# Two transformer blocks on one core: a later read of the bias table, plain float32 sums for the modulation, and the first activation on other engines

## The chip, the cores and the metric

The kernel runs on one core of one Trainium2 chip. The metric is the device time of one execution in microseconds (us). Five engines work beside each other, each in its own order: PE (TensorE, matrix products; the loading of its weights is listed as PEld), DVE (VectorE), ACT (ScalarE), POOL (GpSimd) and SP (SyncE, which here only issues transfers). ACT also issues a few transfers.

## The reference

Two blocks over 256 tokens of width 2048, all in float32. What the change touches is the head of the first block:

```python
c_act = jax.nn.silu(c)
mod = c_act @ w_ada[l] + b_ada[l]                     # 6 * 2048 columns
sh1, sc1, gt1, sh2, sc2, gt2 = jnp.split(mod, 6, axis=-1)
h = modulate(rms_norm(x, g_mix[l]), sh1, sc1)         # y * (1 + scale) + shift
z = h @ w_in[l]                                       # eleven parts
o_sb = stick_breaking_attention(...)
o_ds = indexer_sparse_attention(..., rel_bias)        # 8 heads
```

In the sparse attention an indexer of 16 heads scores all keys, the best 64 per query are kept, and every head adds a bias that depends on the distance of query and key (a table of 32 buckets). Then follow the output projections, a feed-forward part with a short convolution, and a second block with forgetting attention, sparse attention in three branches and a gated feed-forward part.

## The kernel before

**Weights.** All weights come once, in float32, in loads of up to 128x1024 elements (512 KB) that SP issues into a ring of `raw` buffers (line 268 for weights, line 271 for the modulation matrix `w_ada`). There are ten such buffers in the first projection and six from its last part on. A load of weights is split in two: ACT rounds it into a high half `wh` (line 295), DVE subtracts that from it to give the low half `wl` (line 302). Every product is then three passes on PE (high by high, high by low, low by high; lines 402 to 407 and 418 to 420), with the activation split in the same manner. The splitting runs three half-loads ahead of PE's products.

**Order.** The order of the work is written out by the program itself. A function `run` goes through the list of loads and emits the products; after every 1.27 us worth of matrix columns it makes one *tick*, which lets every running generator (norms, attention heads, modulation sums) emit its next step. `yield` in a generator waits for the next tick, `wait(n)` for n of them. So a later tick is a later place in every engine's queue.

**Modulation.** `mod` is computed in 28 chunks of 2 to 4 times 128 columns. The rows of `w_ada` are multiplied by `cact` and summed over the k-tiles, partly by DVE (line 329), partly by ACT and POOL (lines 326, 327), into two accumulators. The first two chunks go another way: plain float32 products on PE (lines 320 and 354). For the other 26 `ada_finish` (line 361) runs over several ticks: POOL adds the two accumulators (line 366), two ticks later ACT rounds the sum into a high half (line 368), a tick later DVE makes the low half (line 370), and 3 or 10 ticks after that PE sums over the partitions by multiplying with a column of ones (line 375), two products per 128 columns. `ada_put` (line 347) adds the bias of the layer.

**First activation.** The 16 k-tiles of `x` are handled in six parts of 2, 2, 3, 3, 3 and 3 (`KG`). The first projection goes over these parts one after the other, and adds the results of a part to those of the parts before: in turn DVE adds out of PSUM (lines 524, 526) or ACT copies (line 521) and POOL adds (line 522). While part j is multiplied, `h_prep(j + 1)` makes the next: `h_scale` multiplies by the norm factor `rb` (line 632, DVE), then it waits until the modulation columns are there, forms the gain (line 641, DVE), applies gain and shift per k-tile (line 645, DVE), and one tick later each ACT (line 656) and DVE (line 659) make the two halves.

**Bias table.** When the eight heads of the first attention are done, three generators start in the same tick: `bias_table`, `indexer` and `ds_chain` (line 1053). `bias_table` gathers the table, and at its end ACT issues one transfer that writes it to memory 128 times over (line 772, tile `tabs`, 8 x 128 x 384 elements, 1.57 MB, in rows of 1536 bytes). `ds_chain` waits until that generator has emitted its last step, then issues the read for head 0 (line 779, `bias_rows`, from ACT), waits for the indexer and starts the heads (`ds_head`, POOL adds the bias in lines 904 and 905). The indexer emits one head per tick (PE lines 803 and 804, ACT line 807, DVE line 813), then the selection of the best keys; it takes some 60 ticks.

Of the kernel before, what the change touches and what calls it, by code (L numbers as in the profile page):

```python
# [9 lines left out]
F32 = mybir.dt.float32  # L10
# [28 lines left out]
RA = (0.6, 0.7, 0.9, 0.9, 0.45)  # L39
GAPS = (5, 7)  # L40
KG = (2, 2, 3, 3, 3, 3)
KG0 = tuple(sum(KG[:j]) for j in range(len(KG)))
# chunks of the modulation's columns, (first, number), in units of 128
ADA = [(16 * m + k, n) for m in (0, 1) for k, n in zip(KG0, KG)] + [(c, 4) for c in range(32, 96, 4)]
# [77 lines left out]
def kernel(ctx: ExitStack, tc: tile.TileContext, t):  # L122
# [29 lines left out]
    invp = const.tile([128, 1], F32, name="invp")  # L152
    onesr = const.tile([128, 2], F32R, name="onesr")
    cact = const.tile([128, 16], F32, name="cact")
# [10 lines left out]
    class Pair:  # L165
        """an activation [128 * nk, T] as two parts whose sum it is, the two of a k-tile beside each other"""

# [11 lines left out]
        def part(self, i, k0, n):  # L179
            """high or low parts of k-tiles of one slot"""  # L180
            return self.slots[k0 // 4].rearrange("p (k i) n -> p i k n", i=2)[:, i, k0 % 4:k0 % 4 + n, :]
# [11 lines left out]
    def lut(func, **kw):  # L193
        """an activation of a table function; Exp and Ln out of the set that has both"""
        if func in (AF.Exp, AF.Ln) and tables[0] != "ln_exp":
            nc.scalar.add_instruction(mybir.InstLoadActFuncSet(
                name=nc.get_next_instruction_name(), act_func_set_id=LN_EXP, engine=mybir.EngineType.Activation,
                ins=[], outs=[]))
            tables[0] = "ln_exp"
        elif func not in (AF.Exp, AF.Ln):  # L200
            tables[0] = func
        nc.scalar.activation(func=func, **kw)  # L202

    # ---------------------------------------------------------------- stream of weights
    P = {}
# [28 lines left out]
    def pieces(n, width):  # L234
        """(first, number) of the k-tiles of every piece that a raw buffer holds"""
        m = -(-n // (RAW // width))
        return [(n * i // m, n * (i + 1) // m - n * i // m) for i in range(m)]
# [46 lines left out]
    def split(idx, g, ks, off, stage):  # L284
        """parts of a weight half, or of the modulation: what ScalarE does, then what VectorE does"""
        it, r = items[idx], raw_of[idx]
# [74 lines left out]
    def ada_finish(a):  # L361
        acc, w = ada_acc.pop(a), 128 * ADA[a][1]
        s = acc[:, 1, :w]
        hl = P.get("ft", ab).tile([128, 2, 512], F32R, name="adahl", tag="adahl", bufs=1)
        yield
        nc.gpsimd.tensor_tensor(out=s, in0=acc[:, 0, :w], in1=s, op=OP.add)
        yield from wait(2)
        nc.scalar.activation(out=hl[:, 0, :w], in_=s, func=AF.Copy)
        yield
        nc.vector.tensor_sub(out=hl[:, 1, :w], in0=s, in1=hl[:, 0, :w].bitcast(F32))  # L370
        yield from wait(FW[a // NKG if a < 2 * NKG else 2])
        ps = psm()
        for j in range(ADA[a][1]):
            for x in range(2):
                nc.tensor.matmul(ps[:, 2 * j:2 * j + 2], hl[:, x, 128 * j:128 * (j + 1)], onesr, start=(x == 0),
                                 stop=(x == 1))
        ada_put(a, ps, 2)

# [115 lines left out]

    # ---------------------------------------------------------------- helpers
    def alt():
# [11 lines left out]
    def gather(out_, ps):  # L508
        """the sum of a bank's halves"""
        nc.scalar.activation(out=out_, in_=ps[:, :T], func=AF.Copy)  # L510
        nc.vector.tensor_add(out=out_, in0=ps[:, T:], in1=out_)
# [36 lines left out]
    def rsqrt_of(out_, src, inv_n, w):  # L548
        """out = 1/sqrt(src * inv_n + eps)"""
        r0 = tmp.tile([128, T], F32, name="r0", tag="r0", bufs=1)[:, :w]  # L550
        m = tmp.tile([128, T], F32, name="mm", tag="mm", bufs=1)[:, :w]
        lut(out=r0, in_=src, func=AF.Ln, scale=inv_n, bias=epsc)
        lut(out=r0, in_=r0, func=AF.Exp, scale=-0.5)
        nc.vector.tensor_scalar(out=m, in0=src, scalar1=inv_n, scalar2=EPS, op0=OP.mult, op1=OP.add)
        nc.vector.tensor_mul(out=m, in0=m, in1=r0)
        nc.vector.tensor_mul(out=m, in0=m, in1=r0)
        nc.vector.tensor_scalar(out=m, in0=m, scalar1=-0.5, scalar2=1.5, op0=OP.mult, op1=OP.add)
        nc.vector.tensor_mul(out=out_, in0=r0, in1=m)
# [3 lines left out]

    # ---------------------------------------------------------------- block 1, attention
    poolA = ExitStack()
# [26 lines left out]
    nc.vector.memset(invp, 1.0 / 128)  # L591
    nc.scalar.activation(out=onesr, in_=ones[:, 0:2], func=AF.Copy)
    lut(out=cact, in_=V["c"], func=AF.Silu)
# [34 lines left out]

    def h_scale(j):
        for _, b, u, m in h_segs(j):  # L630
            x = xt[b][:, u, :]
            nc.vector.tensor_tensor(out=x, in0=x, in1=rb[:, None, :].to_broadcast([128, m, T]), op=OP.mult)

    def h_prep(j):
        """the modulated norm, k-tiles of part j"""
        k0, n = KG0[j], KG[j]
# [6 lines left out]
        for k in range(k0, k0 + n):  # L643
            x = xt[k // 8][:, k % 8, :]
            nc.vector.tensor_scalar(out=x, in0=x, scalar1=gain[:, k:k + 1], scalar2=mod[:, k:k + 1], op0=OP.mult,
                                    op1=OP.add)
            if j == 0:
                nc.scalar.activation(out=acts["h"](k)[0], in_=x, func=AF.Copy)
        if j == 0:
# [28 lines left out]

    # stick-breaking attention, one head
    def sb_head(h):  # L680
# [34 lines left out]
    def av_out(a, vs, o_pair, h, extra=None):  # L715
        """o^T = sum over sources of v^T a, with a in [keys, q] blocks"""
        O = psm()
# [21 lines left out]
    def seq(gens, gap):  # L739
        """start the generators one after the other, gap ticks apart, and go on until all are done"""  # L740
        mine = []
# [16 lines left out]

    # relative-position bias: bias_h[p, u] = table_h[127 - p + u], out of a copy of the table for every p
    tabs = dram.tile([8, 128, 384], F32, name="tabs")  # L760
# [20 lines left out]

    # indexer
    kix = ab.tile([128, T], F32, name="kix")
# [77 lines left out]
    def scores(q, k):  # L861
        """S[q, keys] = q^T k"""
        S = psm()
# [4 lines left out]
    def softmax(S, add, pool, shift=None):  # L868
        """p[q, keys] = exp(S + add + shift - max), with row sums"""
        p = pool.tile([128, 384], F32, name="t2", tag="t2")  # L870
# [48 lines left out]

    # ---- groups of block 1  # L920
    def f_evac(name, base, first=True, scale=None):
# [12 lines left out]
    def f_groups(tiles, nk, act, rmap, **kw):  # L934
        """groups of up to four feature tiles, each (weights, column, what takes its result)"""
        gs = []
# [116 lines left out]
    def ds_chain():  # L1053
        while gens["bias"] in active:
            yield
        rows_of[0] = bias_rows(0)
        while gens["ix"] in active:
            yield
        yield from seq([ds_head(h) for h in range(8)], GAPS[1])

# [76 lines left out]

    # ---------------------------------------------------------------- block 1, output projection and FFN
    def open_ffn(first):
# [14 lines left out]
    def x_out(k, g_ap, pair, accs):  # L1154
        """scaled copy of x chunk k as operand pair, and sums of squares"""
        x = xk(k)
# [208 lines left out]

    # ---------------------------------------------------------------- block 2, mixer
    R = {}
# [23 lines left out]
    def head_norm(z, gname, w=512):  # L1391
        """z[128, w] /= rms over the partitions, times the gain"""
        g = R["gcol"][:, GC[gname]:GC[gname] + 1]
# [52 lines left out]
    def ctok(j):  # L1446
        """kc or vc, and after its two heads the position embeddings of a block's halves"""
        return R["ck"].rearrange("p a n -> p (a n)")[:, 544 * j:544 * j + 544]
# [39 lines left out]
    def compress():  # L1488
        """weights of a block's halves beside each other times a row of every chunk, then the chunks' sums"""
        ws = {}  # L1490
# [38 lines left out]

    # compressed branch, all heads at once  # L1530
    def cmp_branch():
# [71 lines left out]

    # forgetting attention
    vf = get("vf", lambda: ring.tile([128, 2, 1024], F32, name="ringv", tag="ring"))
# [98 lines left out]

    # ---------------------------------------------------------------- block 2, output projection and FFN
    def on_act(k):
# [85 lines left out]
```

## Time and profile before

| what | us |
|---|---|
| three runs | 2840.61, 2840.67, 2844.85 |
| median | 2840.67 |
| span of the profiled execution, first to last instruction | 2837.6 |
| PE busy | 2732.4 (96%) |
| DVE busy | 2030.4 (72%) |
| ACT busy | 1431.9 (50%) |
| POOL busy | 831.5 (29%) |
| transfers | 590.45 MB, mean 208 GB/s |

The profiled execution's own time is not given apart from its span; the span leaves out what lies before the first and after the last instruction. A matmul's end is modelled, and products overlap, so a PE that is shown as busy can still lose time between them. [...] All times in the profile count from the first instruction.

### The profile page before, as it was taken

The page shows a single profiled execution, that of the slowest core. Times are in us where ns is not written, and L with a number is a line of the kernel's source. Part 1 is how long each engine was busy: PE and PEld are TensorE (multiplying, and loading weights), DVE is VectorE, ACT ScalarE, POOL GpSimd, SP SyncE. Part 2 cuts the span into 40 slices and gives each one's busy share as a digit, 9 for nine tenths or more (in the row PEclk, how much of TensorE's full clock was granted, in tenths as well). Part 3 has the DMA queues.
Part 4 walks back from the last instruction along what each step waited for, and adds up shares of the span by engine and source line. Part 5 has one row for each costly group of instructions (what it writes and reads, how often), then busy time and mean ns, then how long its engine had stood idle before and what let it go on. Part 6 is the DMA issues. An engine that isn't in the chain of part 4 may idle for free.

```text
span 2837.6 us, 47798 instructions
## 1 busy us (share of the span) xinstructions
PE 2732.4 (96%) x18364; PEld 2494.8 (88%) x18364; DVE 2030.4 (72%) x2851; ACT 1431.9 (50%) x2138; POOL 831.5 (29%) x703
## 2 busy tenths in 40 slices
PE   7899996989999999999999999999999999999999
PEld 7788885788988999989999888989998888888888
DVE  8999994988888996555666774676775665556654
ACT  5554563555655655434454543555554454344443
POOL 3766751456664541000101210111222221012210
PEclk9999998999999999999999999999999999999999
DMA  9787766778977875655555576544555555555554
GB/s 325 240 258 239 240 219 170 251 232 270 305 259 248 282 268 180 192 188 184 184 183 184 181 214 194 163 128 132 188 186 187 189 181 193 186 187 189 188 194 141
DMA packets 334944, 590.45 MB, mean 208 GB/s; under 512 B 21234, under 2 KB 85594, under 8 KB 334716
## 3 DMA queue, kind: packets, MB, share of 16 engines
q1 hardware_dynamic: 331236, 583.61, 63.3%
q10 hardware_dynamic: 3480, 3.79, 0.7%
q8 instruction: 144, 2.36, 0.3%
q14 instruction: 84, 0.69, 0.1%
HBM read 581.49 MB, written 5.78 MB: 207 GB/s over the span
## 4 chain that ended last, share of the span: by engine, by line
PE 67%; DVE 4%; DMA 2%; issue 2%; ACT 2%; POOL 1%; DVEq 0%; ACTq 0%; SPq 0%; POOLq 0%
PE pg L403 24%; PE pg L402 12%; PE pg L405 8%; PE pg L406 8%; PE pg L407 8%; DVE wl L302 2%; PE pg L399 1%; PE pm L732 1%; PE pg L418 1%; ACT wh L295 1%; PE pg L420 1%; PE pg L419 1%; PE pg L400 1%; DVE adaacc L329 1%; PE pm L1503 1%
## 5 line engine op out<-in xcount | busy, mean ns | idle before, releaser
L302 DVE TENSOR_TENSOR wl<-raw,wh 128x1024 fp32r<-128x1024 f32 (+1 forms) x921 | 1185.9, 1299 | 665.9 <-ACT wh L295 660.3
L295 ACT ACTIVATE wh<-raw 128x1024 fp32r<-128x1024 f32 (+2 forms) x922 | 933.7, 1026 | 843.7 <-PE pg L403 503.2
L403 PE MATMUL pg<-ring,wh 128*128 128x512 f32 x3384 | 1204.6, 397 | 0.0
L402 PE MATMUL pg<-ring,wl 128*128 128x256 f32 x3384 | 958.6, 283 | 1.8 <-DVE wl L302 1.8
L405 PE MATMUL pg<-ring,wh 128*128 128x256 f32 (+1 forms) x2828 | 814.3, 288 | 14.2 <-DVE ring L1096 4.9
L407 PE MATMUL pg<-ring,wl 128*128 128x256 f32 (+1 forms) x2828 | 800.6, 283 | 15.7 <-DVE wl L302 15.4
L406 PE MATMUL pg<-ring,wh 128*128 128x256 f32 (+1 forms) x2828 | 804.3, 284 | 3.7 <-DVE ring L659 3.7
L403 PEld LDWEIGHTS pg<-ring,wh 128*128 128x128 f32 x3384 | 638.9, 189 | 141.4
L402 PEld LDWEIGHTS pg<-ring,wl 128*128 128x128 f32 x3384 | 638.9, 189 | 17.0 <-issue 5.0
L405 PEld LDWEIGHTS pg<-ring,wh 128*128 128x128 f32 x2828 | 538.8, 191 | 24.5 <-issue 9.1
L407 PEld LDWEIGHTS pg<-ring,wl 128*128 128x128 f32 x2828 | 541.8, 192 | 20.2 <-DVE wl L302 20.2
L406 PEld LDWEIGHTS pg<-ring,wh 128*128 128x128 f32 x2828 | 539.6, 191 | 7.8 <-DVE ring L659 4.4
L327 POOL TENSOR_TENSOR adaacc<-raw,adaacc 128x512 f32<-128x512 f32 (+2 forms) x152 | 231.5, 1523 | 270.0 <-ACT raw L326 205.1
L537 POOL TENSOR_TENSOR ring<-gy,ring 128x256 fp32r<-128x256 f32 x88 | 107.0, 1230 | 663.7 <-ACT ring L535 663.7
L329 DVE SCALAR_TENSOR_TENSOR adaacc<-raw,cact,adaacc 128x512 f32<-128x512 f32 (+2 forms) x228 | 223.7, 985 | 2.7 <-DMA raw<-in_w_ada 1.1
L1271 POOL TENSOR_TENSOR gy<-ga,rb 128x256 f32<-128x256 f32 x44 | 53.5, 1226 | 331.3 <-ACT ga L202 331.3
L326 ACT ACTIVATE raw<-raw,cact 128x512 f32<-128x512 f32 (+2 forms) x152 | 102.9, 680 | 51.3 <-DMA tabs<-t 31.6
L522 POOL TENSOR_TENSOR ring<-pt,ring 128x256 f32<-128x256 f32 x95 | 108.3, 1150 | 53.8 <-ACT pt L521 52.9
L1166 POOL TENSOR_TENSOR ssq<-ssq,sq 128x256 f32<-128x256 f32 x60 | 64.4, 1087 | 141.7 <-ACT sq L1164 140.5
L1409 POOL TENSOR_TENSOR hm<-hm,hsq 128x512 f32<-128x512 f32 (+1 forms) x15 | 18.3, 1223 | 286.7 <-ACT hsq L202 286.7
L399 PE MATMUL pg<-ring,wh 128*128 128x512 f32 x200 | 81.5, 408 | 4.8 <-DVE ring L1172 3.0
L418 PE MATMUL pg<-wh,ring 128*128 128x512 f32 (+3 forms) x236 | 83.1, 352 | 0.0
(302 smaller groups left out, 2698.1 us busy)
## 6 DMA issues: line engine op xcount, KB each, us to landing
raw<-in_w_in SPq DMA_DIRECT2D x240, 512.0 KB, 4.6
raw<-in_w_gate SPq DMA_DIRECT2D x176, 512.0 KB, 4.3
raw<-in_w_up SPq DMA_DIRECT2D x176, 512.0 KB, 4.5
raw<-in_w_down SPq DMA_DIRECT2D x176, 512.0 KB, 4.1
raw<-in_w_ada SPq DMA_DIRECT2D x144, 512.0 KB, 5.1
raw<-in_w_out SPq DMA_DIRECT2D x64, 512.0 KB, 4.3
raw<-in_w_ada SPq DMA_DIRECT2D x64, 384.0 KB, 4.0
raw<-in_w_o_sb SPq DMA_DIRECT2D x16, 512.0 KB, 5.1
```

What stands on the lines that cost most here:

```text
L295: nc.scalar.activation(out=hi, in_=src, func=AF.Copy)
L302: nc.vector.tensor_sub(out=lo, in0=src, in1=hi.bitcast(F32))
L327: nc.gpsimd.tensor_tensor(out=acc, in0=x, in1=acc, op=OP.add)
L329: nc.vector.scalar_tensor_tensor(out=acc, in0=x, scalar=cs, in1=acc, op0=OP.mult, op1=OP.add)
L399: nc.tensor.matmul(g.ps[f], hi[:, fs], both, start=True, stop=False)
L402: nc.tensor.matmul(ps, lo[:, fs], xh, start=False, stop=False)
L403: nc.tensor.matmul(g.ps[f], hi[:, fs], both, start=False, stop=stop)
L405: nc.tensor.matmul(ps, hi[:, fs], xh, start=start, stop=False)
L406: nc.tensor.matmul(ps, hi[:, fs], xl, start=False, stop=False)
L407: nc.tensor.matmul(ps, lo[:, fs], xh, start=False, stop=stop)
L418: nc.tensor.matmul(ps, xh[:, bs], hi, start=start, stop=False)
L522: nc.gpsimd.tensor_tensor(out=y, in0=x, in1=y, op=OP.add)
```

## The change

The bias table's first read is put 45 ticks later. The modulation sums lose their split in halves: PE multiplies the float32 sum of the two accumulators by a float32 column of ones, 3 ticks earlier after POOL's addition than before. For parts 1 to 5 of the first activation POOL multiplies by the norm factor, and ACT applies gain and shift; part 0 stays as it was. The diff also takes out comments, which are left out here.

```diff
+LAND = 45
...
-    onesr = const.tile([128, 2], F32R, name="onesr")
...
     def ada_finish(a):
         acc, w = ada_acc.pop(a), 128 * ADA[a][1]
         s = acc[:, 1, :w]
-        hl = P.get("ft", ab).tile([128, 2, 512], F32R, name="adahl", tag="adahl", bufs=1)
         yield
         nc.gpsimd.tensor_tensor(out=s, in0=acc[:, 0, :w], in1=s, op=OP.add)
-        yield from wait(2)
-        nc.scalar.activation(out=hl[:, 0, :w], in_=s, func=AF.Copy)
-        yield
-        nc.vector.tensor_sub(out=hl[:, 1, :w], in0=s, in1=hl[:, 0, :w].bitcast(F32))
         yield from wait(FW[a // NKG if a < 2 * NKG else 2])
         ps = psm()
         for j in range(ADA[a][1]):
-            for x in range(2):
-                nc.tensor.matmul(ps[:, 2 * j:2 * j + 2], hl[:, x, 128 * j:128 * (j + 1)], onesr, start=(x == 0),
-                                 stop=(x == 1))
-        ada_put(a, ps, 2)
+            nc.tensor.matmul(ps[:, j:j + 1], s[:, 128 * j:128 * (j + 1)], ones[:, 0:1], start=True, stop=True)
+        ada_put(a, ps, 1)
...
-    nc.scalar.activation(out=onesr, in_=ones[:, 0:2], func=AF.Copy)
...
     def h_scale(j):
+        eng = nc.gpsimd if j else nc.vector
         for _, b, u, m in h_segs(j):
             x = xt[b][:, u, :]
-            nc.vector.tensor_tensor(out=x, in0=x, in1=rb[:, None, :].to_broadcast([128, m, T]), op=OP.mult)
+            eng.tensor_tensor(out=x, in0=x, in1=rb[:, None, :].to_broadcast([128, m, T]), op=OP.mult)
...
         for k in range(k0, k0 + n):
             x = xt[k // 8][:, k % 8, :]
+            if j:
+                nc.scalar.activation(out=x, in_=x, func=AF.Identity, scale=gain[:, k:k + 1], bias=mod[:, k:k + 1])
+                continue
             nc.vector.tensor_scalar(out=x, in0=x, scalar1=gain[:, k:k + 1], scalar2=mod[:, k:k + 1], op0=OP.mult,
                                     op1=OP.add)
-            if j == 0:
-                nc.scalar.activation(out=acts["h"](k)[0], in_=x, func=AF.Copy)
+            nc.scalar.activation(out=acts["h"](k)[0], in_=x, func=AF.Copy)
...
     def ds_chain():
         while gens["bias"] in active:
             yield
+        yield from wait(LAND)
         rows_of[0] = bias_rows(0)
```

## Rows read from the trace of the kernel before

**Rows 1.** Windows: stretch, then busy us and count per engine, PEclk, DMA share, GB/s.

```profile
480.00:490.00 10.00, 0.00 (x0) 0.00 (x0) 0.00 (x0) 0.00 (x0) 0.00 (x0) 0.50 0.46 64
500.00:510.00 10.00, 10.00 (x45) 7.00 (x43) 9.86 (x18) 5.66 (x11) 3.62 (x2) 0.88 0.74 232
```

**Rows 2.** Timeline 455 to 530: start, us, engine, line, tiles; idle before in brackets.

```profile
461.44 1.30 ACTq L772 DMA_DIRECT2D tabs<-t  x1
494.91 0.72 ACT L326 ACTIVATE raw<-raw,cact 128x512 f32<-128x512 f32 x1 [31.55 <-DMA tabs<-t]
497.00 0.79 PE L803 MATMUL pm<-kix,ring 64*128 64x128 f32 x2 [23.36 <-ACT t L807]
```

**Rows 3.** Timeline of PE 500 to 510, the indexer's heads.

```profile
501.44 0.79 PE L803 MATMUL pm<-kix,ring 64*128 64x128 f32 x2
506.81 0.49 PE L803 MATMUL pm<-kix,ring 64*128 64x128 f32 x2
509.25 0.48 PE L803 MATMUL pm<-kix,ring 64*128 64x128 f32 x2
```

**Rows 4.** Windows again, 70 to 380.

```profile
70.00:380.00 310.00, 280.77 (x1933) 257.68 (x1932) 298.92 (x393) 168.00 (x307) 218.56 (x186) 0.97 0.75 246
```

**Rows 5.** Waits of PE, 0 to 470: us in total, times, longest.

```profile
PE pg L407 <- DVE wl L302: 14.9, 17, 2.4
```

**Rows 6.** Line 268, 440 to 460, then the load at 463.8.

```profile
DMA to landing us min/median/max: 3.4/5.2/5.5
...
L268 SPq DMA_DIRECT2D raw<-in_w_in x1: 368/368/368, 463.8 to 463.8; - x1
DMA to landing us min/median/max: 19.1/19.1/19.1
```

**Rows 7.** DMA queues 464 to 478, then 478 to 483, then 483 to 496.

```profile
q10 hardware_dynamic: 468, 0.72, 45.0%
q1 hardware_dynamic: 145, 0.28, 6.4%
...
q1 hardware_dynamic: 127, 0.24, 12.6%
...
q10 hardware_dynamic: 476, 0.66, 40.1%
```

**Rows 8.** Timeline of SP: the last weight load before the table is written.

```profile
457.54 0.37 SPq L268 DMA_DIRECT2D raw<-in_w_in  x1
```

**Rows 9.** Groups of DVE, 70 to 380: count, busy us, mean ns, idle.

```profile
L370 DVE TENSOR_TENSOR adahl<-adaacc,adahl 128x384 fp32r<-128x384 f32 (+1 forms) x9 | 8.5, 945 | 0.0
L632 DVE TENSOR_TENSOR ring<-ring,rb 128x768 f32<-128x768 f32 (+2 forms) x6 | 6.9, 1183 | 0.0
L645 DVE TENSOR_SCALAR ring<-ring,gain,mod 128x256 f32<-128x256 f32 x12 | 5.7, 529 | 0.1
```

**Rows 10.** Group of POOL by line and form, 20 to 400.

```profile
L522 POOL TENSOR_TENSOR ring<-pt,ring 128x256 f32<-128x256 f32 x94 | 107.5, 1154 | 52.1 <-ACT pt L521 51.3 <-DMA raw<-in_w_ada 0.4
```

**Rows 11.** Line 302 on DVE by form: 70 to 380, then 2200 to 2800.

```profile
L302 DVE TENSOR_TENSOR wl<-raw,wh 128x1024 fp32r<-128x1024 f32 x64 | 96.0, 1500 | 1.6 <-ACT wh L295 1.3 <-DMA raw<-in_w_in 0.3
...
L302 DVE TENSOR_TENSOR wl<-raw,wh 128x1024 fp32r<-128x1024 f32 x214 | 264.5, 1245 | 229.7 <-ACT wh L295 229.1
```

**Rows 12.** Line 1159: ACT Identity with a scale, ns min/median/max.

```profile
L1159 ACT ACTIVATE ring<-ring,gain x32: 492/496/512, 814.3 to 1660.1; 128x256 fp32r<-128x256 f32 x32
```

**Rows 13.** PE timeline: line 375, then line 320.

```profile
1064.52 0.95 PE L375 MATMUL pm<-onesr,adahl 128*128 128x2 f32 x8
...
17.62 3.25 PE L320 MATMUL pm<-cact,raw 128*128 128x1 f32 x28
```

**Rows 14.** Timeline of POOL at 149 and of PE at 154: one modulation sum.

```profile
149.63 1.33 POOL L366 TENSOR_TENSOR adaacc<-adaacc 128x384 f32<-128x384 f32 x1 [2.41 <-DVE adaacc L329]
...
154.84 0.17 PE L375 MATMUL pm<-onesr,adahl 128*128 128x2 f32 x1
```

**Rows 15.** Timeline of PE at 789, the sum that is waited for at once.

```profile
789.17 0.37 PE L375 MATMUL pm<-onesr,adahl 128*128 128x2 f32 x1 [2.49 <-ACT adahl L368]
```

## The prediction

> **What bounds the kernel now.** I first read the page's forty slices and then the windows of ten microseconds, looking for stretches in which PE does nothing. One stands out: from 480 to 490 no engine works at all, and the granted clock is 0.50 there, the lower of its two levels (1.2 GHz), and still 0.88 on average from 500 to 510 [rows 1]. The timeline tells why. ACT issues the write of the bias table at 461.44 (line 772). The next thing in its queue that needs it, the first bias read of line 779, waits for the write to land, and everything behind it on ACT waits too: ACT's next instruction starts at 494.91 after 31.55 us of idling, and PE, which needs ACT's copy of an indexer head, starts at 497.00 after 23.36 [rows 2]. The first step after that takes 501.44 - 497.00 = 4.44 us where later ones take 509.25 - 506.81 = 2.44 [rows 3], so the low clock costs some 2 to 2.6 us more (the second step is late as well). The stop costs **26 us** in all.
>
> The second stretch is 70 to 380, parts 1 to 5 of the first projection. PE is busy 280.8 of 310 us, DVE 298.9, ACT 168.0, POOL 218.6 [rows 4]. PE waits there for DVE's low halves of the weights, 14.9 us in 17 waits [rows 5]: DVE is the bound, and PE has 310 - 280.8 = 29 us to gain.
>
> **The bias read (part 1 of the change).** It takes nothing away; it puts 45 ticks of the schedule between write and read. A tick is 1.27 us of matrix columns in the code. With an indexer head in it, it takes 2.44 us [rows 3]; twelve heads are left after the write, so the read comes about 12 x 2.44 + 33 x 1.27 = 71 us after it, near 532. In the trace the write has landed by 494.9. The indexer needs 60 ticks from its start, the table 8 and the wait 45, so the read is issued 7 ticks, 9 us, ahead of the first head that adds it, against 5.2 us for a load of weights [rows 6]. ACT's wait of 31.55 us goes, and as the read finds its data it holds up nothing behind it on ACT.
>
> What is late next? The write itself goes on for 33 us, now beside the weight stream. The one load that SP issued in its course, at 463.8, took 19.1 us to land, where the five before took 5.2 [rows 6]. The queue rows show how: in 464 to 478 the weights' queue got 145 packets through, then **none** until 478; from 478 to 483 the other 127; from 483 to 496 the write went on alone with 476 [rows 7]. The write held about half the engines (45.0% of sixteen), in two blocks, and the half of a load that falls to those engines passed between the blocks. I take it that one load passes there and the later ones wait for the end. [...]
>
> Then PE runs on after 473.6, the point where it stopped (497.00 - 23.36), with the weights that had landed. Loads for the projection alternate with loads for the modulation, so of the last five before the write only two carry weights (one stands in [rows 8]). Each feeds two heads' steps, 2 x 2.44 = 4.9 us, so PE runs to 483.4. The load of 463.8 lands at 482.9 and needs about 2.3 us on ACT and DVE: 1.8 us idle. It lasts to 490.1. The next weights land some 2.6 us after the write's end at 494.3 and are split by 499.4: 9.3 us idle. With the low clock's 2 to 2.6 us the cost is about 13 in place of 26: **gain 13 us**. If all loads pass between the blocks the whole 26 comes; if none does before a much longer write ends, it turns into a loss. These are the ends.
>
> **The first activation (part 3).** On DVE six instructions of line 632 (6.9 us), twelve of line 645 (5.7) and, from part 2 of the change, nine of line 370 (8.5) leave this stretch: 21.1 us [rows 9]. Onto POOL come the six, over 12 k-tiles; the nearest row is line 522, 1154 ns for a 128x256 addition [rows 10], so 13.8 us on an engine that is idle for 91 of 310. Does POOL's work cost DVE time? Line 302's 128x1024 takes 1500 ns here and 1245 late in the kernel, where POOL does little [rows 11]: 17% of DVE's 299 us, 51 us, beside 219 us of POOL, or 0.23 per us. By that row the new work costs DVE 3.2 us, and at most all of its 13.8. I take 8, between them, because an instruction of 2 or 3 k-tiles is longer than those on which the row rests: gain 21.1 - 8 = **13 us**, from 7 to 18, within PE's 29. A cover that could fail is POOL's own queue: its additions for the evacuated sums stand behind the moved scaling; if that stalled ACT's evacuation by one scaling of 3.5 us in each of four parts, the gain would be gone, so nothing is the lower end.
>
> ACT gets twelve Identity instructions of about 496 ns [rows 12], 6 us, and loses nine copies of like length: no cost beside 142 us of idling. They wait for the gain of line 641, which DVE computes late; behind them on ACT stand the weights' high halves, but these run ahead of DVE, which waits for that same gain.
>
> **The modulation sums (part 2).** Before, eight matmuls of two columns for four sums took 0.95 us. A float32 matmul shows as two records: in line 320, 28 of them took 3.25, 0.116 each against 0.119 [rows 13]. 92 sums make 184 records either way: no cost. The copy and the subtraction go (and the copy of ones at the start, where ACT waits for x anyway: nothing), and with them three ticks, 3.8 us. In the example POOL's sum ended at 149.63 + 1.33 = 150.96 and PE took it at 154.84, 3.9 us later [rows 14]; now PE arrives as POOL ends. I cost that at nothing: a wait of up to 2.5 us per sum is possible, but PE is ahead of DVE there and would only wait elsewhere. One sum is on the path: at 789 PE stood 2.49 us for ACT's copy [rows 15]. **Gain 2 us**, between 0 and 6.
>
> **Sum.** 13 + 13 + 2 = 28. The traced execution has a span of 2837.6 us; its own time is not shown apart, and the runs' median, 2840.67, lies 3.1 above that span. I take the same off both: span 2809.6, time 2840.7 - 28 = **2812.7**.
>
> **Rivals.**
> *The write hides wholly.* Loads queued at 478 all pass between the two blocks: 26 + 13 + 2 = 41, 2799.7. For it: nothing shows that a second load would have to wait. Against: the write took the engines back by 483. Chance 0.26.
> *POOL's work costs DVE as much as it saves.* DVE waits all 13.8 us and part of the rest goes in POOL's queue; the first projection gains 3 at most: 13 + 3 + 2 = 18, 2822.7. For it: line 302's 20% stretch; against: POOL has room. [...] Chance 0.18.
> *The stop only moves.* The 45 ticks pass sooner than counted, or the write lands later than 532, and ACT stands at line 779 again: about 13 + 2 = 15, 2825.7. Chance 0.04.
> *Slower: the write starves the weights.* Beside the stream the write itself takes longer, and no load passes on its engines. PE runs dry at 490 as before; with a write of 80 us it would resume near 546, at a cost of 60 us in place of 26: 2840.7 + 34 - 15 = 2860. It decides from a write of about 60 us, where the 15 of the other parts are used up. Against it: a load did pass. Chance 0.04.
>
> **Numbers.** The forecast has 0.48. Its own ends are 12 to 26 for the read, 0 to 18 for the activation. The range reaches from the hidden write with an activation gain of 18 (2795) to the port case with nothing gained there and no gain in the sums (2828); the slower case is left out. No change that is under 0.2%, 5.7 us, can be told from none here. Faster takes every case but the slow one, less 0.03 for their worst ends: 0.93; same 0.03; slower 0.04.
>
> **What would show it.** Right: no wait of ACT for the table; PE idle near 484 and 490 for some 11 us, with weight loads of 464 to 480 landing after 494; DVE still busy over 93% but PE's busy share from 70 to 380 above 0.93, and that stretch 13 us shorter; line 302 there at 1500 ns or a little more. Wrong: no PE gap around 490 (the write hides), line 302 at 1600 or more (the port), PE waiting for line 366 by more than 5 us in sum, or ACT still waiting on the table.

## The result and the profile after

The kernel after takes **2816.09 us** (median of four runs, 2812.5 to 2818.41) against 2840.64 for the kernel before in the same comparison, so 24.6 us or 0.86% faster by the medians. The ratio on record is 0.9900, with an interval of 0.9889 to 0.9912; the quotient of the medians, 0.9914, lies just outside it, and by the ratio itself the gain would be 28 us. The record does not say how the ratio weighs the runs; the text goes by the medians throughout. The forecast was 2812.7 in a range of 2795 to 2828.

| what | us after |
|---|---|
| the profiled execution's own time | 2818.41 (the slowest of the four) |
| its span | 2816.6 (before: 2837.6) |
| PE, DVE busy | 2734.5 (97%), 2007.7 (71%) |
| ACT, POOL busy | 1424.9 (51%), 841.1 (30%) |
| transfers | 590.45 MB, mean 210 GB/s |

**The stop is gone.** The timeline of ACT around the table's write, and the line of the first bias read with its landing (us):

```profile
458.34 1.28 ACTq L768 DMA_DIRECT2D tabs<-t  x1
459.29 0.95 ACT L803 ACTIVATE t<-pm 128x384 f32<-128x384 f32 x2
460.13 0.72 ACT L327 ACTIVATE raw<-raw,cact 128x512 f32<-128x512 f32 x1
...
L775 ACTq DMA_DIRECT2D bt<-tabs x1: 357/357/357, 554.2 to 554.2; - x1
...
DMA to landing us min/median/max: 2.4/2.4/2.4
```

The instruction behind the write starts at once, where it stood for 31.55 us before [rows 2]. The read is issued 96 us after the write and finds its data. The windows that answer to [rows 1] show PE at work throughout, but not at full share, and the granted clock at 0.83 in the two that hold its longest gaps:

```profile
480.00:490.00 10.00, 9.40 (x46) 6.29 (x46) 6.56 (x14) 4.61 (x11) 1.51 (x1) 1.00 0.77 177
490.00:500.00 10.00, 7.88 (x43) 6.23 (x43) 5.37 (x8) 4.43 (x7) 3.09 (x2) 1.00 0.77 250
500.00:510.00 10.00, 7.42 (x34) 6.18 (x33) 9.86 (x16) 5.18 (x7) 4.58 (x3) 0.83 0.52 173
510.00:520.00 10.00, 8.32 (x49) 6.86 (x47) 9.86 (x20) 4.66 (x8) 3.17 (x2) 1.00 0.95 314
520.00:530.00 10.00, 7.41 (x34) 6.46 (x35) 9.86 (x23) 5.07 (x7) 5.03 (x4) 0.83 0.83 256
```

**Where the time came from, and where some went back.** I lined up the same matmuls of two traces, by tile and order. The table gives how much earlier (minus) the matmuls of a stretch start than in the kernel before, in the median and in us, for the profiled execution of each kernel; the columns are times of the kernel before, and the kernels are those of the next section. Each row is one execution, and the runs of a kernel differ by up to 9 us (e2) and 6 us (the kernel after), so differences of a few us between rows are read together with the times.

| kernel | 370 to 380 | 500 to 520 | 555 to 575 | 800 to 840 | end |
|---|---|---|---|---|---|
| after | -3.3 | -29.0 | -18.8 | -22.4 | -21.0 |
| e1, read alone | 1.7 | -24.1 | -17.9 | -15.5 | -15.9 |
| e2, sums alone | -10.1 | -9.3 | -8.5 | -9.4 | -12.8 |
| e5, read and sums | -7.4 | -33.3 | -22.9 | -24.0 | -25.7 |
| e7, e5 and ACT's part | -4.5 | -30.2 | -19.3 | -21.7 | -24.1 |
| e8, e5 and a wider write | -8.9 | -34.8 | -33.1 | -35.0 | -35.3 |

In the kernel after, the first projection gives only 3.3 us. The stop then gives 26 us, as the prediction had counted it, and some 10 of them are lost again by 555.

What takes them back are late loads. In the kernel after, the loads for the projection that SP issues from 460 to 480 (line 269, with their landing) answer to [rows 6]; DVE's timeline then shows the waits for the high halves of these loads, and PE's timeline what it pays, later, when DVE is behind (it is busy 9.86 of 10 us in each window from 500 to 530):

```profile
L269 SPq DMA_DIRECT2D raw<-in_w_in x4: 367/3764/4416, 460.7 to 478.7; - x4
...
DMA to landing us min/median/max: 17.8/20.2/24.1
```

```profile
481.92 1.23 DVE L303 TENSOR_TENSOR wl<-raw,wh 128x1024 fp32r<-128x1024 f32 x1 [8.52 <-ACT wh L296]
490.99 1.23 DVE L303 TENSOR_TENSOR wl<-raw,wh 128x1024 fp32r<-128x1024 f32 x1 [2.51 <-ACT wh L296]
496.34 2.02 DVE L303 TENSOR_TENSOR wl<-raw,wh 128x1024 fp32r<-128x1024 f32 x1 [1.73 <-ACT wh L296]
...
498.41 0.39 PE L396 MATMUL pg<-ring,wl 128*128 128x256 f32 x1 [2.12 <-DVE wl L303]
508.43 0.39 PE L396 MATMUL pg<-ring,wl 128*128 128x256 f32 x1 [2.58 <-DVE wl L303]
514.59 0.39 PE L396 MATMUL pg<-ring,wl 128*128 128x256 f32 x1 [1.48 <-DVE wl L303]
549.86 0.38 PE L399 MATMUL pg<-ring,wh 128*128 128x256 f32 x1 [2.09 <-DVE ring L505]
```

The name in the bracket is ACT, but ACT itself waits: in 455 to 600 its longest sum of waits is for these transfers:

```profile
ACT wh L296 <- DMA raw<-in_w_in: 29.5, 11, 8.3
```

Two of these waits, on ACT's timeline, end while the table is still being written (to 493.5):

```profile
480.83 1.06 ACT L296 ACTIVATE wh<-raw 128x1024 fp32r<-128x1024 f32 x1 [8.26 <-DMA raw<-in_w_in]
489.90 1.06 ACT L296 ACTIVATE wh<-raw 128x1024 fp32r<-128x1024 f32 x1 [3.61 <-DMA raw<-in_w_in]
```

SP was slower as well: the instructions that issue these four loads took 3.76 us in the median and up to 4.42 (the second and third figure of the line for 269, in ns), where the last one before the write took 0.37 in the kernel before [rows 8]. What held SP was not tried.

**The first projection.** DVE's, POOL's and ACT's groups there (70 to 377 after; they answer to [rows 9] and [rows 11]), then who DVE waited for in 60 to 380 (us in total, times, longest):

```profile
L303 DVE TENSOR_TENSOR wl<-raw,wh 128x1024 fp32r<-128x1024 f32 x65 | 98.8, 1520 | 8.3 <-ACT wh L296 8.3
...
L626 POOL TENSOR_TENSOR ring<-ring,rb 128x768 f32<-128x768 f32 (+2 forms) x6 | 10.0, 1688 | 0.0
...
L640 ACT ACTIVATE ring<-ring,mod,gain 128x256 f32<-128x256 f32 x12 | 6.4, 592 | 3.6 <-DVE gain L635 3.5
...
DVE wl L303 <- ACT wh L296: 10.2, 7, 2.3
```

In the kernel before that last wait was 3.5 us in 5. The timelines of ACT and of DVE at 186 show one of the places:

```profile
186.00 1.59 ACT L640 ACTIVATE ring<-ring,mod,gain 128x256 f32<-128x256 f32 x3
187.49 1.56 ACT L296 ACTIVATE wh<-raw 128x1024 fp32r<-128x1024 f32 x2
...
185.67 0.29 DVE L635 SCALAR_TENSOR_TENSOR gain<-mod,vec 128x3 f32<-128x3 f32 x1
188.57 1.83 DVE L303 TENSOR_TENSOR wl<-raw,wh 128x1024 fp32r<-128x1024 f32 x2 [1.57 <-ACT wh L296]
```

DVE finishes the gain at 185.96, ACT then runs three Identities, and only behind them in its order stands the high half that DVE needs next. There are five such gaps in the five parts, 9.2 us in all.

### The profile page after: what moved, and what is told of

Its sections match the earlier page's. It is cut to its first block, busy times and chain, and to the rows that moved or that the text cites. A ratio compares the mean times of both kernels' runs of the same rounds, so it can differ in the third digit from the quotient of the medians.

```text
span 2816.6 us, 47791 instructions
## 1 busy us (share of the span) xinstructions
PE 2734.5 (97%) x18364; PEld 2496.7 (89%) x18364; DVE 2007.7 (71%) x2804; ACT 1424.9 (51%) x2124; POOL 841.1 (30%) x710
## 2 busy tenths in 40 slices
DMA packets 334944, 590.45 MB, mean 210 GB/s; under 512 B 21234, under 2 KB 85594, under 8 KB 334716
## 4 chain that ended last, share of the span: by engine, by line
PE 76%; DVE 10%; DMA 5%; issue 4%; POOL 3%; ACT 2%; SPq 0%; DVEq 0%; ACTq 0%; POOLq 0%
PE pg L397 25%; PE pg L396 13%; PE pg L399 9%; PE pg L400 9%; PE pg L401 9%; DVE wl L303 4%; DVE adaacc L330 3%; PE pg L393 2%; DMA raw<-in_w_in 2%; PE pm L728 1%; PE pg L412 1%; ACT wh L296 1%; PE pg L414 1%; PE pg L413 1%; DMA raw<-in_w_out 1%
## 5 line engine op out<-in xcount | busy, mean ns | idle before, releaser
L401 PE MATMUL pg<-ring,wl 128*128 128x256 f32 (+1 forms) x2828 | 799.9, 283 | 13.9 <-DVE wl L303 13.8
L401 PEld LDWEIGHTS pg<-ring,wl 128*128 128x128 f32 x2828 | 541.4, 191 | 17.8 <-DVE wl L303 17.8
L330 DVE SCALAR_TENSOR_TENSOR adaacc<-raw,cact,adaacc 128x512 f32<-128x512 f32 (+2 forms) x228 | 234.2, 1031 | 3.6 <-DMA raw<-in_w_ada 2.0
```

The source lines that it names most:

```text
L330: nc.vector.scalar_tensor_tensor(out=acc, in0=x, scalar=cs, in1=acc, op0=OP.mult, op1=OP.add)
L401: nc.tensor.matmul(ps, lo[:, fs], xh, start=False, stop=stop)
```

## The experiments

All were timed against the kernel before (2841.96 us beside e1 to e4, 2839.43 beside e5 to e8, 2841.44 beside e9 and e10), with 4 to 12 runs of each. The third column is the difference of the medians, the last the ratio on record.

| run | time, us | below before | ratio, interval |
|---|---|---|---|
| e1 read alone | 2822.64 | 19.3 | 0.9929 (0.9915 to 0.9942) |
| e2 sums alone | 2831.06 | 10.9 | 0.9960 (0.9946 to 0.9974) |
| e3 scale on POOL alone | 2840.90 | 1.1 | 0.9995 (0.9986 to 1.0003) |
| e4 Identity on ACT alone | 2841.44 | 0.5 | 0.9992 (0.9982 to 1.0003) |
| e5 read and sums | 2811.17 | 28.3 | 0.9896 (0.9881 to 0.9911) |
| e6 e5 and scale on POOL | 2811.04 | 28.4 | 0.9896 (0.9880 to 0.9911) |
| e7 e5 and Identity on ACT | 2815.73 | 23.7 | 0.9913 (0.9898 to 0.9928) |
| e8 e5, table written from 16 rows | 2803.87 | 35.6 | 0.9870 (0.9855 to 0.9885) |
| e9 whole change, Identities later | 2814.67 | 26.8 | 0.9904 (0.9887 to 0.9921) |
| e10 e9, table written from 16 rows | 2807.73 | 33.7 | 0.9880 (0.9865 to 0.9895) |

**e1, the later read alone** (on the kernel before).

```diff
+        yield from wait(45)
         rows_of[0] = bias_rows(0)
```

> The kernel before with the later bias read alone. Theory: the stop of 26 us goes, but some 11 us of it are given back between 490 and 560, because the loads of weights that SP issues beside the table's write land 15 to 24 us after their issue (5 before), DVE idles for them and is then the bound until the selection of keys is done. So about 14 us faster (11 to 17), no wait of ACT for the table, and loads that land late. Rival (the write hides, and what is given back comes from the other parts of the change): 24 us faster or more.

It was worth 19.3 us, more than the theory's 11 to 17 and less than the rival's 24; the interval reaches from 16.5 to 24.2 us and so settles neither by itself. Its row in the table of shifts shows that some is given back without the other parts: 25.9 us won by 500 (from +1.7 to -24.1), 6.2 lost by 555 and 8.6 by 800.

**e2, the plain sums alone.** The parts of the change in `ada_finish` and the column of ones, nothing else.

```diff
-        nc.scalar.activation(out=hl[:, 0, :w], in_=s, func=AF.Copy)
...
-        nc.vector.tensor_sub(out=hl[:, 1, :w], in0=s, in1=hl[:, 0, :w].bitcast(F32))
...
+            nc.tensor.matmul(ps[:, j:j + 1], s[:, 128 * j:128 * (j + 1)], ones[:, 0:1], start=True, stop=True)
```

> The kernel before with the plain float32 sums alone (no split of the sums, three ticks earlier). Theory: nine of the 26 subtractions lie in the first projection, where DVE is the bound, so most of their 8.5 us come back, and 2 us at the sum that is waited for at once: about 9 us faster (5 to 12). Rival (PE now waits for POOL's addition, 12.5 us in nine waits in the changed kernel, and this eats the gain): within 3 us of before.

10.9 us, as the theory had it. In the profiled execution ten of them come in the first projection, where the relief of DVE is paid out; that execution was the fastest of the six, 4.3 us under their median. In the kernel after, PE does stand for POOL's addition at these sums, as this line of line 370 in 60 to 1000 shows (us, times), but that did not eat the gain:

```profile
POOL adaacc L366: 12.5, 9
```

**e3, the norm factor on POOL alone, and e4, gain and shift on ACT alone.**

```diff
     def h_scale(j):
+        eng = nc.gpsimd if j else nc.vector
```

> The kernel before with the norm factor on POOL alone, for parts 1 to 5. Theory: DVE loses 6.9 us of work from 70 to 380, and its other operations with two operands in SBUF grow by about as much beside POOL's new 10 us: between 3 us faster and 3 us slower. Rival (the port is not the matter): 6 to 7 us faster.

```diff
+            if j:
+                nc.scalar.activation(out=x, in_=x, func=AF.Identity, scale=gain[:, k:k + 1], bias=mod[:, k:k + 1])
+                continue
```

> The kernel before with gain and shift on ACT alone, for parts 1 to 5. Theory: DVE loses 5.7 us of work, but ACT does its three Identity instructions per part between DVE's gain and the next high halves of the weights, so that DVE idles about 1.8 us per part for them, 9 us in all: 0 to 5 us slower. Rival (ACT's high halves run ahead of DVE and nothing waits): 5 us faster.

Neither can be told from no change. For e4 that decides nothing: its interval reaches from 5.1 us faster to 0.9 slower, and so touches both the theory's band and the rival's. For e3 the groups of POOL and DVE in 70 to 377 say why:

```profile
L633 POOL TENSOR_TENSOR ring<-ring,rb 128x768 f32<-128x768 f32 (+2 forms) x6 | 9.6, 1619 | 0.0
...
L302 DVE TENSOR_TENSOR wl<-raw,wh 128x1024 fp32r<-128x1024 f32 x64 | 99.8, 1559 | 1.6 <-ACT wh L295 1.6
L329 DVE SCALAR_TENSOR_TENSOR adaacc<-raw,cact,adaacc 128x384 f32<-128x384 f32 x80 | 78.5, 981 | 1.1
```

Line 302 took 1500 ns before [rows 11] and line 329 took 949: 64 x 59 ns + 80 x 32 ns = 6.3 us more on DVE, against the 6.9 that left it [rows 9]. Of these, the 2.6 us of line 329 are less sure, as that line took 981 ns in e2 too, with nothing new on POOL. In the same two lines e6 has 6.8 us more than e5, and the whole change 7.0 more than e7. So DVE paid 6.3 us for the 9.6 us of POOL. By what means is not shown; "the port", in the forecast and in the expectation of e3, is the author's name for this cost.

**e5, read and sums together; e6 and e7, one of the other two parts added to that.** The edits are those above.

> The change without its third part: later bias read and plain sums, the first activation as before. Theory: the parts add, and the third part takes back about 7 us of what the sums gain in the first projection: 30 us faster than before (27 to 33), some 5 us faster than the whole change. Rival (the read and the sums overlap, and the third part is worth nothing either way): 24 to 25 us faster.

> The change without ACT's part: late read, plain sums, norm factor on POOL, gain and shift on DVE. Theory (ACT's part is what costs, as DVE idles for high halves behind it): about as without the third part, 28 to 31 us faster than before. Rival (POOL's part is what costs, through the operands that both read from SBUF): 24 to 26 us faster.

> The change without POOL's part: late read, plain sums, norm factor on DVE, gain and shift on ACT. Theory (ACT's part is what costs): 24 to 27 us faster than before, DVE idle about 9 us more than without it between 60 and 380. Rival (POOL's part is what costs): 29 us or more.

e5 and e6 came as expected and equal. e7, 23.7 under the kernel before where the theory had 24 to 27, lost 4.6 us against e5: all four runs of e7 (2815.29 to 2817.94) lie above all four of e5 (2808.9 to 2813.75) and of e6 (2807.38 to 2814.2). DVE's waits in 60 to 380, first in e5, then in e7:

```profile
DVE wl L301 <- ACT wh L294: 2.7, 4, 1.1
```

```profile
DVE wl L301 <- ACT wh L294: 9.1, 7, 2.3
```

DVE's idle time there rose from 11.1 to 20.6 us while 5.7 us of its work had gone, and in the table of shifts 2.9 us of the loss are there at 370 to 380 (-7.4 and -4.5). In e4 it rose in like manner, from 9.8 in the kernel before to 18.7, with the same work gone, and the time stayed as it was.

**e8, e5 with the table written from 16 rows.** Each row of the table is made twice and each copy is written 64 times in place of 128; the memory holds the same.

```diff
-        nc.tensor.matmul(ps[:8, :384], relb, oh, start=True, stop=True)
+        nc.tensor.matmul(ps[:16, :384], relb2.rearrange("p h a -> p (h a)"), oh, start=True, stop=True)
...
-        nc.scalar.dma_start(out=tabs, in_=tb[:, None, :].to_broadcast([8, 128, 384]))
+        nc.scalar.dma_start(out=tabs.rearrange("h (a c) u -> (h a) c u", a=2),
+                            in_=tb[:, None, :].to_broadcast([16, 64, 384]))
```

> Late read and plain sums as in the kernel without the third part, and the table is written from 16 rows of the source instead of 8 (each row of the bias twice, 64 copies of each), so that sixteen engines write it, 64 rows each. Theory (9 to 11 us are given back because the loads of weights wait behind the write on half of the engines): the write lasts about 17 us instead of 33, DVE idles less beside it, and 4 to 8 us more are gained. Rival (what is given back is DVE's own bound in the selection of keys, whatever the loads do): no change against the kernel with the write on 8 engines. Worse is possible too: if all sixteen engines hold the loads up at once, PE runs dry for a few us.

7.3 us better than e5, all four runs (2803.51 to 2804.21) below all of e5's. The DMA queues of e8 in 454 to 468:

```profile
q10 hardware_dynamic: 890, 1.37, 89.6%
q1 hardware_dynamic: 17, 0.02, 0.4%
```

The write holds twice the share of the engines (89.6%, against 44.4% in the kernel after) for half the time (17 us against 33.7), and hardly any weights pass while it runs (17 packets). Yet the loads for the projection are less late (8.6 to 17.3 us from issue to landing in 453 to 471, against 17.8 to 24.1 in the kernel after in 460 to 480), and DVE waits less for them. DVE's low halves in 460 to 520 with their idle time, in e5 and then in e8:

```profile
L301 DVE TENSOR_TENSOR wl<-raw,wh 128x1024 fp32r<-128x1024 f32 x11 | 17.1, 1553 | 14.0 <-ACT wh L294 14.0
```

```profile
L302 DVE TENSOR_TENSOR wl<-raw,wh 128x1024 fp32r<-128x1024 f32 x14 | 21.0, 1498 | 6.1 <-ACT wh L295 6.1
```

In the table of shifts e8 keeps what the read wins (-34.8, then -33.1), where e5 gives back 10 us. Only the write and the small steps that make its rows differ, so the give-back is shown to come from it.

**e9, the whole change with the Identities two ticks after the gain; e10, that with the 16-row write.**

```diff
+        if j:
+            yield from wait(2)
         for k in range(k0, k0 + n):
```

> The whole change with one more edit: two ticks between the gain (VectorE) and ScalarE's twelve Identities, so that high halves of weights go ahead of them on ScalarE and the gain is there when they come up. Work and engines as in the whole change. Theory 1, the wait in ScalarE's queue costs the 4 us that the whole change lost against the version without it: ScalarE's idle time before the Identities (3.6 us) goes, VectorE's waits for high halves in 60 to 380 fall from 10.2 us to under 6, its idle time from 19 to under 14, and the time falls by 3 to 5 us against the whole change: 26.5 to 28.5 under the kernel before, ratio 0.990. Theory 2, ScalarE's added 6 us of work or the later high parts of the activation cost it, not the wait: VectorE's waits stay near 10 us and the time stays 23 to 25.5 under the kernel before, ratio 0.9912 or more.

> The run above with the bias table written from 16 rows in place of 8. Theory 1, the write's price and the wait's price are separate: 7 us less than the run above, as the 16-row write took off the read with the sums, so 33 to 36 under the kernel before. Theory 2, with the write short the first projection's gain is not passed on (the two overlap in what VectorE catches up): less than 4 us under the run above. If the Identities' delay does not help, 30 to 32.5 under the kernel before.

In e9 ACT's idle time before its Identities went from 3.6 us to 0.0, DVE's wait for high halves fell from 10.2 to 6.3 and its idle time from 19.2 to 14.8. Both just miss the bounds set for theory 1. The time, 26.8 under the kernel before, is in its band, but its interval holds the whole change's ratio too. In e10, with the same delay, the wait for high halves is 5.9 us, but DVE's idle time is 18.5, near the whole change's 19.2. So the delay takes away part of the wait for high halves; that this gains time is not shown, and theory 2 stays open. e10 gave 6.9 us more than e9, as expected; e8, without POOL's and ACT's parts, has the lowest median, 35.6 under the kernel before against 33.7, but the two intervals overlap. The interval of e8 lies below that of the whole change, so e8 beats both kernels.

## Why the prediction was right, and where it was wrong

The forecast of 28 us met 24.6 us. Split by edit, it had 13 for the read; 2 + 8.5 for the sums with their share of DVE's relief [rows 9]; 6.9 - 8 = -1.1 for the scaling; and 5.7 for gain and shift. The runs give these four as 17.4 (e5 less e2), 10.9 (e2), 0.1 to 1.1 (e6 less e5, and e3; the whole change less e7 gives 0.9) and -4.6 (e7 less e5; the whole change less e6 gives -3.8). Each is a difference of medians whose own intervals reach 2 to 5 us to either side.

**The read: right in what it removes, too low in what it gives.** ACT's wait went, and the 26 us of the stop were all won at first. The step "later ones wait for the end" of the write failed; it was the author's estimate, and no run of the write from 8 rows shows it. It rested on [rows 7]: no weights passed from 483 to 496, and I took the write for a lock. But no load stood in the queue then. SP had issued one in that time, the prediction says so itself, and 0.28 + 0.24 MB, one load of 512 KB, were through by 483. SP's timeline of the kernel before has the next issue at 497, and the write's own line in 478 to 483, which [rows 7] leave out, shows that there were no two blocks with a pause between them either:

```profile
463.77 0.37 SPq L268 DMA_DIRECT2D raw<-in_w_in  x1
497.06 0.37 SPq L271 DMA_DIRECT2D raw<-in_w_ada  x1
...
q10 hardware_dynamic: 158, 0.24, 36.8%
```

The write moved 158 packets in those 5 us, 32 per us, nearly as before (468 in 14 us, 33 per us), while the second half of the load went through beside it. The queues of the kernel after, 464 to 475 and then 475 to 493, have loads waiting throughout:

```profile
q10 hardware_dynamic: 349, 0.54, 44.4%
q1 hardware_dynamic: 272, 0.52, 18.2%
...
q1 hardware_dynamic: 1066, 2.07, 36.4%
q10 hardware_dynamic: 533, 0.82, 36.0%
```

In the write's second half 2.07 MB, almost four loads, went through beside it, and the write nearly kept its pace (349 packets in 11 us, 533 in 18). So the forecast's gaps of PE near 484 and 490, 11 us together, are not there: PE is busy 9.40 of 10 us from 480 to 490 and 7.88 from 490 to 500. The loads still landed late, after 14.7 to 24.1 us against 5.2 [rows 6], because little passed in the write's first half; DVE ran out first, 14.7 us in the four gaps of its timeline between 473 and 497 (three of them are above), and PE paid in smaller pieces up to 550. The price of the write was 7 to 9 us (19.3 in e1, 17.4 in e5 less e2, of 26 were kept), not 13; a gain of 13 lies outside e1's interval. The read was also issued 96 us after the write where the sum of ticks gave 71, which changed nothing, as it found its data.

**The sums: right in size.** 10.5 by the forecast's terms, 10.9 measured. One of the forecast's own signs of being wrong did appear here: PE waits for line 366 for 12.5 us in sum, where it had set a limit of 5. The forecast put these waits at nothing, as PE would only wait elsewhere, and the time of e2 agrees with that.

**The scaling: right.** DVE pays for POOL's work nearly what it saves. The 8 us taken for it was near the 6.3 to 7.0 of e3, e6 and the whole change; the bound of 13.8 was not reached, and POOL's work was 10.0 us. Line 303 took 1520 ns, as foreseen; more of the price fell on line 330 in the whole change (1033 ns against 976 in e7), which the forecast did not look at.

**Gain and shift: wrong, by 10 us.** The failed step is "no cost beside 142 us of idling", with its reason that the high halves "run ahead of DVE". They don't run far enough ahead: at 186 DVE needs the one that stands right behind the Identities. It was also wrong that a wait of both engines for the same gain would cancel: DVE makes the gain itself, so ACT starts after it, and DVE has the next subtraction to do at once. ACT's idle share could not show that; its order does. e7 shows it as a loss of 4.6 us, about what 9.5 us more of idle time less 5.7 of work leave. That the order in ACT's queue, and not ACT's added work, makes all of this loss is argued from the trace and not shown: e9 did not settle it. e4, with nearly the same new idle time but without the sums' relief, shows no loss that its interval can tell; why not was not tried.

So the total came out only 3.4 us short by the medians (by the ratio on record, not short at all), in part by luck, as errors of opposite sign partly cancelled: +4.4 for the read, -10.3 for gain and shift, +0.4 and about +2 for the rest. The stretch of the first projection shows it: it was to be 13 us shorter, with PE busy over 93%, and in the profiled execution it was 3.3 us shorter by the table, with PE busy 280.5 of 307 us (91%).

No rival took place as it was told: the write did not hide wholly, ACT did not stand for the table again, and nothing was starved. The second came near in part: the first projection gained about its 3 us, and POOL's work cost DVE about what it saved, but the 13.8 us of waiting were not there, and the loss came from ACT's part.

## What to carry to other kernels

An idle stretch of a transfer queue in the trace says that a bigger transfer shuts it out only if something stood in the queue; look at the issues before reading it as a lock (here SP issued none between 463.77 and 497.06). An operation moved to an engine with idle time can still cost (4.6 us in e7), if something behind it in that engine's order is due before it is done; the moment to look at is the one where the producer of its input is also the next consumer. Where a transfer holds half the engines, spreading it over all of them can be better for a stream beside it, though it stops the stream for a while: in e8 it gave 7.3 us, with 17 packets of weights through in 14 us.

## What the runs showed of the hardware

**The write's width.** From 8 rows the table's transfer held 44 to 45% of sixteen engines in its first half (36.0% in 475 to 493, beside the weights) and lasted from 459.8 to 493.5 in the kernel after; from 16 rows it held 89.6% and lasted 17 us in e8.

**Weights beside the write.** In e8 17 packets of weights passed in 14 us beside 890 of the write. From 8 rows, in the kernel after, fewer passed in the first half (272 packets in 464 to 475, 25 per us) than in the second (1066 in 475 to 493, 59 per us), and loads of the projection were in use from 480.83 and from 489.90, before the write's end at 493.5. Why the second half is shared more was not tried.

**The clock.** The clock column is the share of PE's full clock that was granted; the records of the kernel before hold two values, 0.50 and 1.00. At 0.50 matmuls of 256 columns start 0.213 us apart (lines 405 to 407, six of them from 107.18 to 108.46), so 1.2 columns per ns; at 1.00 they start 0.114 us apart (seven from 1699.92 to 1700.72), so 2.2. The 1.2 GHz of the forecast is the first of these rates, if PE takes a column per cycle, which was not measured.
